# Soft mixture of experts: transposes of x issued from ScalarE's queue, kept operands stored when made

## The chip, the cores and the metric

The kernel runs on one core of a Trainium2 chip. The metric is device time in microseconds (us), from the start of the program to its end. A core has five engines that run side by side, each with its own queue in order: TensorE (PE) multiplies into PSUM, VectorE (DVE) and ScalarE (ACT) compute and empty PSUM, GpSimd (POOL) here does little but issue transfers, and SyncE (SP) only issues transfers. A transfer issued from any queue is carried out by the core's 16 DMA engines.

## The reference

```python
probs = softmax(router_logits)                 # batch 16, seq 512, 8 experts
for e in range(8):
    output += probs[:, :, e:e+1] * (x @ expert_weights[e])   # 512 x 2048 each
```

x has 8192 rows of 512 numbers, the output 8192 rows of 2048 in f32. Each row is weighted by its own probability for each expert, so the sum is one product: the row of x repeated eight times and scaled by the eight probabilities, times the eight experts' weights one above the other.

## The kernel before

That product is computed in f16 by a Strassen-like scheme of seven block products P1 to P7 at the outer level and seven steps (1, 5, 6, 2, 7, 3, 4) inside each. The rows are 32 blocks of 256 (`HQ`), 16 pairs q. The left operand of an outer product (class `Left`, L426) is made by VectorE: `times` (L422) multiplies the transposed block of x (tile xT) with the probabilities broadcast to all partitions (tile pT) into a tile z, and for some products a second such tile is subtracted. TensorE does a step as 8 matmuls of 128 x 128 against 128 x 512 (`mm`, L131). ScalarE copies step results out of PSUM (L541, L545, L548 without a base, L559 with one), VectorE adds the others (L112). In some stages ("Thirds", `run_third`, L820) two steps are split once more, with quarter-size blocks; their copies are L638 and L640.

The work is a list `stages` (L672 on) of one or two outer products each. `run(k)` (L839) goes through the slots of a stage: 7 steps by 1 or 2 products, so 14 slots in a duo stage, and 7 in the one stage that holds P6 of pair 0 alone. VectorE's work stands in a queue of tasks with costs; `slack` (L367) takes tasks off it after each step as long as its modelled clock is behind TensorE's. `need` (L357) pulls a task and all ahead of it when a step asks for its result. The order on each engine is that of the program text, held by `note` and `dve` (L100 to L108).

What concerns the change:

- **x and its transposes** (`XBlock`, L379). `begin` loads 256 rows of x from the input, cast to f16, by GpSimd's queue (tile xs, two chunks of 128 rows), for the stage two ahead, at the end of slot 1. `finish` issues two DMA transposes (L397), one for each chunk, from xs into xT; before the change it is called at the end of slot 7 for the stage two ahead (`after`, L810), from SyncE's queue. `store` writes xT to DRAM for the later passes, at the end of slot 5 of the next stage. Sixty transposes in all, in 30 blocks. Later passes load the stored xT by SyncE.
- **Kept P6 operands** (`Left.store`, L455). For the pairs q = 1 to 13 the two halves of P6's left operand, 512 KB each, are written to DRAM by SyncE and read again for P3 by ScalarE's queue. Before the change a store is issued at slots 1 and 5 of the stage in which P6 runs, which is after the operand was made.
- **SyncE's queue** also has the loads of pT and of stored xT, and the base tiles h (earlier partial sums from the DRAM tiles kept, or from the output). **GpSimd's queue** has the casts of x and of the weights, the parts of weight sums that VectorE builds (wd), and the output stores. **ScalarE's queue** has whole weight tiles (L166) and the kept operands (L492), besides its copies.
- **Pools.** xs, xT and pT share one ring of 9 tiles, the h tiles one of 13; PSUM has 8 banks. A new tile waits until the last use of the buffer that it takes.
- **Semaphores.** Transfers from the hardware queues (SyncE's and ScalarE's together) take eight semaphores in turn in the program's order; a transfer waits until the one before it on its semaphore has landed.

Of the kernel before, what the change touches and what calls it, by code (L numbers as in the profile page):

```python
# [31 lines left out]
def kernel(  # L32
# [7 lines left out]
    nc = tc.nc  # L40
    P = 128
# [337 lines left out]
    class XBlock:  # L379
# [12 lines left out]

        def finish(self):
            if self.xs is not None:
                self.t = xpool.tile([P, C, HQ], f16, name="xT", tag="x")
                for j in range(HQ // P):
                    note(nc.sync.dma_start_transpose(out=self.t[:, :, ds(j * P, P)], in_=self.xs[:, j, :]))  # L397
                self.xs, self.new = None, True

# [6 lines left out]
    class PBlock:  # L406
# [9 lines left out]

        def finish(self):
            pass

        store = finish  # L420

# [4 lines left out]
    class Left:  # L426


        def __init__(self, xb, pb, less=None, of=None, part=None):
            self.xb, self.pb, self.less, self.of, self.part = xb, pb, less, of, part  # L430
            self.t, self.task, self.s2, self.i = [None, None], {}, None, None

# [25 lines left out]
        def queue_make(self, k):  # L458
            for make in self.makes(k):
                self.task[k] = later(1.14, make)  # L460

        def queue_s2(self):
# [303 lines left out]

    def finish_loads(stage):
        if stage < len(stages):
            for p in stages[stage]:
                for load in p.loads:  # L770
                    load.finish()

# [37 lines left out]
    def after(stage, n):  # L810
        if n == 1:
            queue_lefts(stage + 1)
        if n == late.get(stage, 1):
            start_loads(stage + 2)
        if n == 5:
            store_loads(stage + 1)
        if n == 7:
            finish_loads(stage + 2)

# [345 lines left out]
    for q in KEEP:  # L1165
        for k, slot in enumerate((1, 5)):
            at(k5 + 1 + q, slot, lambda q=q, k=k: lefts[6, q].store(k))
        at(k3 + (q - 1) // 2, 8 + 3 * ((q - 1) % 2), lambda q=q: lefts[3, q].part.fetch())
# [14 lines left out]
    store_loads(0)  # L1183
    finish_loads(1)
    for k in range(len(stages)):
# [29 lines left out]
```

## Time and profile before

| | |
|---|---|
| median of 3 runs | 1379.85 us (1375.95 to 1384.18) |
| the profiled execution's own time | 1372.54 us |
| its span in the profile | 1370.8 us |
| granted TensorE clock | 1.0 |
| transfers | 358.50 MB |
| GpSimd's queue (q0), share of the 16 DMA engines | 56.1% |
| SyncE's queue (q1) | 31.3% |
| ScalarE's queue (q10) | 8.3% |

The profile is of one execution. "Busy" is the time in which an engine carried out instructions; those that only issue transfers are listed under the engine's name with a q (SPq, ACTq), and are not busy time. A row of a timeline has start, duration, engine, source line, operation, tiles (out<-in) and a count, and in brackets the idle time before it with what ended it. A row of the waits has total, number and the longest. Line numbers are those of the kernel before.

### The profile page before, as it was taken

The numbers are of one execution on the slowest core, as the hardware profiler recorded it, in microseconds if no ns is written. First come the engines' busy times: TensorE is split into PE (matmuls) and PEld (weight loads), VectorE is DVE, ScalarE is ACT, GpSimd is POOL, SyncE is SP. The second block draws the span as 40 slices with busy tenths as digits, with TensorE's granted clock in tenths as the row PEclk, the third lists the DMA queues.
The fourth block names the chain that finished last, engine by engine and source line by source line (L and its number), as shares of the span: only waits on it lengthen the run. The fifth ranks groups of instructions, "written<-read, shape, count | busy, mean of one in ns | idle before, by whom it ended". The sixth has DMA issues, their size and how long they took to land.

```text
span 1370.8 us, 18076 instructions
## 1 busy us (share of the span) xinstructions
PE 1362.6 (99%) x6610; PEld 644.1 (47%) x6610; DVE 1121.1 (82%) x1359; ACT 193.7 (14%) x354; POOL 411.4 (30%) x652
## 2 busy tenths in 40 slices
PE   8999999999999999999999999999999999999999
PEld 4455444444444444444444444444444444456554
DVE  5868757689889888798887978888889798997873
ACT  3232111100011111111111100000000000123321
POOL 3222333331223343343332112242332422233232
PEclk9999999999999999999999999999999999999999
DMA  9898999999897999999998999889797979999896
GB/s 182 217 223 245 208 237 283 233 323 358 235 340 245 323 295 332 286 318 315 306 296 289 364 371 258 200 236 209 227 264 216 242 212 282 309 209 241 203 207 121
DMA packets 193161, 358.50 MB, mean 262 GB/s; under 512 B 53168, under 2 KB 87216, under 8 KB 187696
## 3 DMA queue, kind: packets, MB, share of 16 engines
q0 software_dynamic: 88688, 185.12, 56.1%
q1 hardware_dynamic: 98336, 130.15, 31.3%
q10 hardware_dynamic: 6048, 42.08, 8.3%
q8 instruction: 51, 0.84, 0.2%
q14 instruction: 38, 0.31, 0.1%
HBM read 214.47 MB, written 170.07 MB: 281 GB/s over the span
## 4 chain that ended last, share of the span: by engine, by line
PE 74%; issue 11%; DMA 9%; POOL 4%; DVE 1%; ACT 0%; SPq 0%; POOLq 0%; DVEq 0%
PE ps L132 74%; DMA out_dram<-h 4%; POOL out_dram L126 2%; DMA wd<-w 2%; DMA xs<-in_x_dram 2%; DMA xT<-xs 1%; POOL wd L126 1%; POOL w L126 1%; DMA w<-in_expert_weights_dram 0%; DVE h L112 0%; DVE z L112 0%; POOL xs L126 0%; SPq L397 0%; POOLq L126 0%; DVE z L234 0%
## 5 line engine op out<-in xcount | busy, mean ns | idle before, releaser
L132 PE MATMUL ps<-w,z 128*128 128x512 f16 (+1 forms) x5272 | 1136.1, 376 | 1.7 <-DMA w<-in_expert_weights_dram 1.2
L132 PEld LDWEIGHTS <-z 128*128 128x128 f16 x5344 | 522.7, 98 | 607.2 <-DVE h L112 1.5
L126 POOL DMA_DIRECT2D out_dram<-h x380 | 249.1, 661 | 722.6 <-ACT h L559 365.4
L112 DVE TENSOR_TENSOR h<-ps,h 128x512 f32<-128x512 f32 x415 | 283.1, 686 | 177.1 <-PE ps L132 159.2
L112 DVE TENSOR_TENSOR z<-xT,pT 128x2048 f16<-128x2048 f16 x220 | 266.8, 1216 | 13.8 <-DMA xT<-xs 11.4
L132 PE MATMUL ps<-w,d 128*128 128x512 f16 x880 | 199.1, 379 | 0.4 <-DVE ps L112 0.4
L132 PEld LDWEIGHTS <-d 128*128 128x128 f16 x880 | 86.1, 98 | 102.5 <-issue 0.7
L112 DVE TENSOR_TENSOR z<-z,d 128x2048 f16<-128x2048 f16 x110 | 131.5, 1215 | 0.0
L112 DVE TENSOR_TENSOR w<-w 128x1024 f16<-128x1024 f16 (+2 forms) x92 | 100.7, 1102 | 9.2 <-DMA wd<-w 5.0
L559 ACT COPY h<-ps 128x512 f32<-128x512 f32 x64 | 37.5, 586 | 480.6 <-PE ps L132 458.8
L548 ACT COPY h<-ps 128x512 f32<-128x512 f32 x90 | 52.8, 586 | 326.5 <-PE ps L132 292.4
L112 DVE TENSOR_TENSOR d<-z 128x1024 f16<-128x1024 f16 x110 | 74.7, 686 | 7.6 <-PE ps L132 6.0
L112 DVE TENSOR_TENSOR ps<-ps,h 128x512 f32<-128x512 f32 (+1 forms) x102 | 60.3, 595 | 19.5 <-PE ps L132 19.3
L545 ACT COPY h<-ps 128x512 f32<-128x512 f32 x90 | 52.0, 589 | 151.7 <-PE ps L132 148.8
L126 POOL DMA_DIRECT2D wd<-w x86 | 48.6, 587 | 45.5 <-DVE w L112 34.7
L126 POOL DMA_DIRECT2D w<-in_expert_weights_dram x65 | 48.4, 761 | 28.0 <-DMA wd<-w 17.9
L126 POOL DMA_DIRECT2D kept<-h x56 | 30.8, 549 | 70.3 <-ACT h L548 40.0
L112 DVE TENSOR_TENSOR z<-z,u 128x2048 f16<-128x2048 f16 x38 | 46.1, 1214 | 0.1
L112 DVE TENSOR_TENSOR u<-xT,pT 128x2048 f16<-128x2048 f16 x38 | 46.2, 1215 | 0.0
L112 DVE TENSOR_TENSOR h<-h 128x512 f32<-128x512 f32 (+2 forms) x69 | 45.0, 674 | 0.1
L541 ACT COPY ps<-ps 128x512 f32<-128x512 f32 x45 | 25.6, 570 | 104.0 <-PE ps L132 98.2
L112 DVE TENSOR_TENSOR z<-z 128x2048 f16<-128x2048 f16 x32 | 39.0, 1220 | 0.6
(60 smaller groups left out, 262.8 us busy)
## 6 DMA issues: line engine op xcount, KB each, us to landing
out_dram<-h POOLq DMA_DIRECT2D x380, 256.0 KB, 6.7
pT<-p_dram SPq DMA_DIRECT2D x127, 256.0 KB, 6.5
w<-wd ACTq DMA_DIRECT2D x27, 1024.0 KB, 9.2
h<-kept SPq DMA_DIRECT2D x100, 256.0 KB, 7.9
xT<-x SPq DMA_DIRECT2D x74, 256.0 KB, 6.6
wd<-w POOLq DMA_DIRECT2D x72, 256.0 KB, 6.2
w<-in_expert_weights_dram POOLq DMA_DIRECT2D x35, 512.0 KB, 9.5
h<-out_dram SPq DMA_DIRECT2D x68, 256.0 KB, 5.5
```

The source lines that it names most:

```text
L112: dve(nc.vector.tensor_tensor(out=o, in0=a, in1=b, op=op))
L126: note(nc.gpsimd.dma_start(out=o, in_=i, **how))
L132: note(nc.tensor.matmul(ps, z, w, start=start, stop=stop, skip_group_check=True))
L541: act(nc.scalar.copy(self.banks["b"], x))
L545: act(nc.scalar.copy(o[tn], q if p == 5 else x))
L548: act(nc.scalar.copy(o[TN[p]], b if p == 2 else x))
L559: act(nc.scalar.copy(o[tn], b))
```

## The change

`finish` issues the transposes one chunk at a time and takes the queue that issues them, ScalarE's unless told otherwise; only the opening's four stay on SyncE's. The first chunk goes out at the end of slot 9 and the second at the end of slot 11 in a duo stage, at 5 and 7 in a stage of one product; before, both went out at the end of slot 7. The store of a kept P6 half becomes a task of cost 0 in VectorE's task queue right behind the one that makes it, so that it is issued where the operand is made.

```diff
-        def finish(self):
+        def finish(self, j, begin=nc.scalar):
             if self.xs is not None:
-                self.t = xpool.tile([P, C, HQ], f16, name="xT", tag="x")
-                for j in range(HQ // P):
-                    note(nc.sync.dma_start_transpose(out=self.t[:, :, ds(j * P, P)], in_=self.xs[:, j, :]))
-                self.xs, self.new = None, True
+                if j == 0:
+                    self.t = xpool.tile([P, C, HQ], f16, name="xT", tag="x")
+                note(begin.dma_start_transpose(out=self.t[:, :, ds(j * P, P)], in_=self.xs[:, j, :]))
+                if j == HQ // P - 1:
+                    self.xs, self.new = None, True
...
         def queue_make(self, k):
             for make in self.makes(k):
                 self.task[k] = later(1.14, make)
+            if self.kept is not None:
+                self.task[k] = later(0.0, lambda: self.store(k))
...
-        if n == 7:
-            finish_loads(stage + 2)
+        first = 9 if len(stages[stage]) == 2 else 5
+        if n in (first, first + 2):
+            finish_loads(stage + 2, (n - first) // 2)
...
-        for k, slot in enumerate((1, 5)):
-            at(k5 + 1 + q, slot, lambda q=q, k=k: lefts[6, q].store(k))
...
-    finish_loads(1)
+    for j in range(HQ // P):
+        finish_loads(1, j, nc.sync)
```

In the order of instructions of the two programs, TensorE, VectorE and GpSimd have the same instructions in the same order. ScalarE gains 56 transposes, SyncE loses them, and SyncE's kept stores stand earlier among its loads.

More of the change, by code (lines that the diff above doesn't have):

```diff
@@ L415, in begin, with finish, store @@
                 sp(self.t, p_dram[self.h, ds(self.first, HE), :].partition_broadcast(P))
-        def finish(self):
+        def finish(self, *how):
             pass
-        store = finish
+        def store(self):
+            pass
     def times(z, k, xb, pb):
@@ L430, in __init__ @@
             self.xb, self.pb, self.less, self.of, self.part = xb, pb, less, of, part
-            self.t, self.task, self.s2, self.i = [None, None], {}, None, None
+            self.t, self.task, self.s2, self.i, self.kept = [None, None], {}, None, None, None
         def makes(self, k):
@@ L765, in start_loads, with finish_loads @@
                     load.begin()
-    def finish_loads(stage):
+    def finish_loads(stage, *how):
         if stage < len(stages):
@@ L770, in finish_loads @@
                 for load in p.loads:
-                    load.finish()
+                    load.finish(*how)
     def store_loads(stage):
```

## Prediction

> **What bounds the kernel now.** I read the page's first part, then TensorE's timeline and its own waits, and only then the queue that the change empties.
>
> ```profile
> span 1370.8 us, 18076 instructions
> PE 1362.6 (99%) x6610; PEld 644.1 (47%) x6610; DVE 1121.1 (82%) x1359; ACT 193.7 (14%) x354; POOL 411.4 (30%) x652
> ```
>
> TensorE is busy for 1362.6 of 1370.8 us. A busy TensorE may still run below its rate, so the next view is its timeline, in one steady stage (14 steps of 8 matmuls) and in the one place where gaps stand.
>
> ```profile
> 640.37 3.62 PE L132 MATMUL ps<-w,d 128*128 128x512 f16 x16
> ...
> 664.54 3.62 PE L132 MATMUL ps<-w,d 128*128 128x512 f16 x16
> ...
> 810.15 3.62 PE L132 MATMUL ps<-w,d 128*128 128x512 f16 x16 [0.41 <-DVE ps L112]
> ```
>
> A stage of 112 matmuls takes 664.54 - 640.37 = 24.17 us, 216 ns a matmul; the row of 16 keeps that rate (16 x 216 ns = 3.46 us, and the tail of the last makes 3.62). A bracket is idle time: none stands in the steady stage, and 0.41 us at 810. The whole list of TensorE's waits:
>
> ```profile
> PE ps L132 <- ACT h L331: 1.4, 1, 1.4
> PE every L94 <- DVE zero L91: 1.3, 1, 1.3
> PE ps L132 <- DMA w<-in_expert_weights_dram: 1.2, 1, 1.2
> PE ps L132 <- DVE h L112: 0.5, 1, 0.5
> PE ps L132 <- DVE ps L112: 0.4, 1, 0.4
> ```
>
> Columns: us in total, times, longest. The first three lie in the opening, before any step that the diff touches. The last two, 0.5 + 0.4 = 0.9 us, come at 810 to 818 us. This is the first bound of the forecast: the change moves no matmul and no VectorE instruction (in the order of instructions, TensorE's, VectorE's and GpSimd's lists are the same before and after), so **in this execution it can give back at most 0.9 us**, 0.07%.
>
> Now SyncE's queue, which the change empties: its wait at the transposes, and the view of line 397 (durations in ns, and how long the transposes took to land).
>
> ```profile
> SPq L397 <- DMA xs<-in_x_dram: 242.5, 23, 17.4
> ```
> ```profile
> L397 SPq DMA_TRANSPOSE xT<-xs x60: 1191/1266/2277, 47.5 to 722.5; - x60
> ...
> DMA to landing us min/median/max: 2.4/6.4/11.3
> ```
>
> SyncE stood 242.5 us at its transposes until the x rows had come, with all its later loads behind it. Yet TensorE waited for none of those loads: the 242.5 us lie beside matmuls.
>
> **The change part by part.**
>
> *Transposes leave SyncE (56 of 60; the first four stay).* Removed there: 56 x 1.266 = 71 us of issuing and the 242.5 us of waiting. On the path: nothing, by the list of TensorE's waits. Cover: the matmuls of the stage. If that cover were thin, the loads queued behind would be late and TensorE's list would show it; after the opening it shows the 0.9 us at 810 alone, past the last transpose (722.5). So 0.
>
> *They go to ScalarE, 2 or 4 at a time.* Added there: 56 x 1.266 = 71 us of issuing on an engine that is busy for 193.7, plus a wait at the head of an in-order queue. What stands behind it: the copies that empty PSUM. I take the worst steady stage that I found, the one in which the rows of x come latest against ScalarE (ScalarE, then SyncE):
>
> ```profile
> 647.47 0.59 ACT L548 COPY h<-ps 128x512 f32<-128x512 f32 x1 [1.14 <-PE ps L132]
> 657.83 0.59 ACT L548 COPY h<-ps 128x512 f32<-128x512 f32 x1 [9.77 <-PE ps L132]
> 661.34 0.57 ACT L541 COPY ps<-ps 128x512 f32<-128x512 f32 x1 [2.92 <-PE ps L132]
> ```
> ```profile
> 651.97 3.17 SPq L397 DMA_TRANSPOSE xT<-xs  x2
> ```
>
> The new transposes stand between the copies of 647.47 and 657.83, in a hole of 9.77 us. ScalarE reaches them at 648.06, waits until 651.97 (3.9 us; SyncE starts there as soon as the rows land), issues two in 2 x 1.266 = 2.5 (3.17 at SyncE) and is free at 654.5 to 655.2, before its next copy at 657.83. Even past that there is room: the first result that TensorE needs is the copy of 661.34, for the second half of the 664.54 row (8 matmuls later, 664.54 + 1.73 = 666.27). Taking off two copies and the issue, 666.27 - 0.57 - 0.59 - 2.5 = 662.6: the rows may land 14.5 us after ScalarE gets there, and land 3.9 after. Price 0.
>
> The tight case is the Third stages near the start, with four transposes and a shorter tail:
>
> ```profile
> 81.36 0.59 ACT L548 COPY h<-ps 128x512 f32<-128x512 f32 x1 [1.14 <-PE ps L132]
> 89.20 0.36 ACT L638 COPY ps<-ps 128x256 f32<-128x256 f32 x1 [7.25 <-PE ps L132]
> ```
> ```profile
> 79.78 14.11 SPq L397 DMA_TRANSPOSE xT<-xs  x4
> ```
> ```profile
> 75.23 1.23 DVE L112 TENSOR_TENSOR z<-xT,pT 128x2048 f16<-128x2048 f16 x1 [6.35 <-DMA xT<-xs]
> ```
>
> 4 x 1.266 = 5.1 us in a hole of 7.25: from 81.95 to 87.0, 2.2 us to spare. Price 0. VectorE gains: SyncE's four took 14.11 us here, with waits between them, where ScalarE takes 5.1; the last row shows VectorE idle for 6.35 us for such a result one stage earlier, which should shrink. It is idle time of VectorE that TensorE did not see, so 0 too.
>
> *Moved later.* In the earlier duo stages SyncE issued its pair ahead of ScalarE's hole; the farthest that I found:
>
> ```profile
> 118.65 3.02 SPq L397 DMA_TRANSPOSE xT<-xs  x2
> ```
> ```profile
> 128.12 0.59 ACT L548 COPY h<-ps 128x512 f32<-128x512 f32 x1 [1.14 <-PE ps L132]
> ```
> ```profile
> 144.48 1.21 DVE L112 TENSOR_TENSOR z<-xT,pT 128x2048 f16<-128x2048 f16 x1
> ```
>
> The pair goes out 10 us later, from 128.71, is issued by 131.2 and lands 6.4 us (median) to 11.3 us (longest) after: 137.6 to 142.5. The first VectorE product that reads it starts at 144.48. Price 0, with 2 us left in the worst case; the store of x and the loads behind it on SyncE are off the path as above.
>
> *Kept P6 operands.* 26 stores of 512 KB, as many as before, now sent when VectorE has made them and not at slots 1 and 5 of the next stage. They get a lane partner: transfers from SyncE's and ScalarE's queues take eight semaphores in turn, and each waits until the last one on its semaphore has landed. The order of instructions with its waits shows that in five stages the second transpose of a pair follows a kept store in this way.
>
> ```profile
> DMA to landing us min/median/max: 4.5/10.3/15.4
> ```
> ```profile
> 592.69 1.23 DVE L112 TENSOR_TENSOR z<-z 128x2048 f16<-128x2048 f16 x1
> ```
> ```profile
> 609.49 0.59 ACT L548 COPY h<-ps 128x512 f32<-128x512 f32 x1 [9.77 <-PE ps L132]
> ```
>
> (The first row is the kept stores', from the view of that tile; then VectorE and ScalarE.) In the latest of the five the operand is ready at 593.9; with the median the store lands at 604.2, with the longest at 609.3, while ScalarE's next copy is at 609.49 and may be some 7 us late unpunished (above: 666.27 - 0.57 - 0.59 - 657.83 = 7.3). Bounds: 0, and 1.3 us of late issue that the same 7 us hide. I take 0. On SyncE the store now waits for VectorE ahead of the base loads; those are added to a product some slots later, and the matmuls cover them again.
>
> *Sum:* -0.9 to 0 against the execution's own 1372.54 us (span 1370.8 and 1.7 around it). I take 0. The runs shown are slower, 1375.95 to 1384.18 with a median of 1379.85, 7.3 above it. No trace shows what those 7.3 us are. With nothing of the sum pointing elsewhere I carry them over: 1379.85 less some of the 0.9, **1379 us**, "no change" within the 0.5% (6.9 us) that a measurement of this kernel can tell.
>
> **The rivals.**
>
> *Slower: the third queue slows GpSimd's transfers.* GpSimd's queue shares the DMA engines with SyncE's; transposes on ScalarE's queue make a third claimant while a pair lands. The place is the stages from 575 to 660 us, where the parts of weights come through GpSimd and VectorE is the one just in time:
>
> ```profile
> 581.32 1.42 DVE L112 TENSOR_TENSOR w<-w 128x1024 f16<-128x1024 f16 x2 [3.97 <-DMA wd<-w]
> ...
> 590.84 0.69 DVE L112 TENSOR_TENSOR ps<-ps,h 128x512 f32<-128x512 f32 x1
> ```
> ```profile
> 592.02 3.62 PE L132 MATMUL ps<-w,d 128*128 128x512 f16 x16
> ```
> ```profile
> DVE w L112 <- DMA wd<-w: 5.0, 3, 4.0
> DVE w L112 <- DMA w<-in_expert_weights_dram: 2.5, 2, 1.8
> ```
> ```profile
> w<-wd POOLq DMA_DIRECT2D x12, 256.0 KB, 5.5
> w<-in_expert_weights_dram POOLq DMA_DIRECT2D x12, 256.0 KB, 9.6
> ```
>
> After a wait of 3.97 us VectorE ends at 591.53 what TensorE uses at 592.02: 0.49 us of margin. If the claimants share evenly and a half becomes a third, a landing of 5.5 or 9.6 us (these two rows are of 480 to 730 us) grows by half, 2.75 to 4.8. VectorE waited for such transfers 3 and 2 times; 3 x 2.75 + 2 x 4.8 = 17.9 us if TensorE feels all, nothing if the pairs miss them. It decides as soon as a part lands over 0.5 us later. Estimate 9, so **1388**. Against it: the transposes' bytes are the same, and in the stage quoted above the pair goes out at its old time, since it waits for the x rows in both kernels; only its company changes.
>
> The Trainium skill, "DMA: Bandwidth & Descriptors", Queues, rings and completion order, has each DMA engine take turns between the queue rows that have work, a packet at a time; by that rule three claimants get a third each, and this rival's time would hold. The same page, under Issuing engines are not separate DMA queues, says that issuing from several engines saves the sequencer's time alone; by it the gain would be SyncE's 71 us of issuing, none of it on the path, and the forecast's time would stand.
>
> *Faster: the runs' 7.3 us are SyncE's late loads.* If the loads behind 242.5 us of waiting are what comes late in executions without a profile, they go, and the kernel falls to its floor: 1372.54 - 0.9 = 1371.6 at best, **1372.5** here. For it: something does vary between executions, and this is the second longest wait in SyncE's list. Against it: TensorE's list has none of it.
>
> *The fixed places are not what holds them.* Where x rows land after ScalarE arrives (651.97 against 648.06), arrival times the transposes in both kernels, and nothing moves: the time of before, **1379.85**.
>
> ScalarE held at the head of its queue also happens in before, where the price can be read:
>
> ```profile
> 795.68 0.59 ACT L559 COPY h<-ps 128x512 f32<-128x512 f32 x1 [14.88 <-DMA w<-wd]
> ```
>
> 14.88 us behind a weight load that it had to issue, and TensorE lost 0.9 us after it at most. A blocked ScalarE is cheap here.
>
> **How the numbers follow.** Forecast 0.57, fixed places that hold nothing 0.11, third queue 0.20, floor 0.10, ScalarE blocked by rows over 14.5 us late 0.02. Within 0.5%: 0.57 + 0.11 = 0.68. Faster by over 0.5% (below 1372.95): 0.10. Slower by over 0.5%: 0.20 + 0.02 = 0.22. The likeliest one's own range is that of the runs, 1376 to 1384. The range that should hold 8 in 10 takes in the floor, 1371.5, and the lower half of the slower rival up to its estimate, 1388.
>
> **What would show it.** Right: TensorE's waits still below 5 us and 24.2 us a steady stage; transposes on ScalarE's queue starting 0 to 10 us later than on SyncE's; no wait of SyncE for xs after the first four; ScalarE's copies after them waiting for TensorE still; VectorE's waits for xT below 11.4 us. Wrong: idle brackets on TensorE between 575 and 660 us with a VectorE releaser that waited for GpSimd's transfers (third queue), brackets released by ScalarE (blocked queue), or timed runs near 1372 (floor).

## The result, and the profile after

The changed kernel takes 1395.94 us in the median of 4 runs (1390.73 to 1400.11), the kernel before on the same chip 1377.9 (4 runs, 1374.63 to 1384.18): ratio 1.0137, 95% interval 1.0111 to 1.0163. That is 18 us slower, outside the predicted range of 1371.5 to 1388. The profiled execution of the changed kernel took 1393.44 us with a span of 1391.7; before it was 1372.54 and 1370.8, so the two profiles differ by 20.9 us. Lines after the change are a few higher: L552 is the copy that was L548, L642 and L644 those that were L638 and L640.

The page's first part, and TensorE's waits (total, times, longest):

```profile
PE 1366.1 (98%) x6610; PEld 644.2 (46%) x6610; DVE 1120.5 (81%) x1359; ACT 193.6 (14%) x354; POOL 412.3 (30%) x652
```
```profile
PE ps L132 <- DVE h L112: 13.4, 5, 8.7
PE ps L132 <- ACT h L644: 3.0, 1, 3.0
PE ps L132 <- DVE ps L112: 2.7, 2, 1.9
```

VectorE and ScalarE do the same work in the same time; TensorE is busy 3.5 us longer with the same matmuls and waits 19.1 us outside the opening where it waited 0.9 (17.6 of them as idle time in brackets). Its timeline says where (start, duration, idle before in the bracket):

```profile
91.89 2.76 PE L132 MATMUL ps<-w,z 128*128 128x512 f16 x16 [1.71 <-DVE h L112]
...
590.85 8.79 PE L132 MATMUL ps<-w,z 128*128 128x512 f16 x40 [1.34 <-DVE h L112]
...
625.92 3.61 PE L132 MATMUL ps<-w,d 128*128 128x512 f16 x16 [1.95 <-DVE ps L112]
...
653.54 10.52 PE L132 MATMUL ps<-w,z 128*128 128x512 f16 x48
672.72 13.29 PE L132 MATMUL ps<-w,z 128*128 128x512 f16 x48 [8.66 <-DVE h L112]
```

Two places: the stages before 320 us (1.71 and 0.77 us around 92, 3.00 at 315), and 590 to 672 us. The largest stop costs more than its 8.66 us: the 48 matmuls behind it take 13.29 us where those ahead of it take 10.52. The view by stretches shows the clock (the column of its own after POOL; then the share of the DMA engines and GB/s):

```profile
672.00:690.00 18.00, 17.28 (x68) 7.26 (x68) 15.91 (x21) 2.24 (x4) 4.51 (x8) 0.82 0.93 245
690.00:702.00 12.00, 12.00 (x57) 5.40 (x56) 8.53 (x13) 1.26 (x3) 4.32 (x8) 1.00 1.01 293
```

The 0.82 is a mean of two: in shorter stretches of the same view the granted clock is 1.00 from 664 to 668 us, 0.51 from 668 to 678 and 1.00 from 680 to 690. So it was halved 4 us into the stop, for 10 us. The Trainium skill, "TensorE: Matmul & The Clock Gate", Part 1: The HAM clock gate, says that an idle window of some 3.4 us drops the clock; the 8.66 us stop agrees with it, and the stops of under 2 us above, and the one of 3.00 us, brought no longer matmuls. In e8, below, a stop of 2.35 us was once enough.

What VectorE waited for, and what GpSimd's queue did ahead of it:

```profile
664.66 0.69 DVE L112 TENSOR_TENSOR w<-w 128x1024 f16<-128x1024 f16 x1 [6.97 <-issue]
668.70 0.69 DVE L112 TENSOR_TENSOR w<-w 128x1024 f16<-128x1024 f16 x1 [3.35 <-DMA w<-in_expert_weights_dram]
671.38 0.69 DVE L112 TENSOR_TENSOR w<-w 128x1024 f16<-128x1024 f16 x1 [1.98 <-DMA w<-in_expert_weights_dram]
```
```profile
649.84 0.54 POOL L126 DMA_DIRECT2D out_dram<-h  x1 [6.77 <-DMA wd<-w]
653.52 0.54 POOL L126 DMA_DIRECT2D out_dram<-h  x1 [3.14 <-DMA wd<-w]
656.90 0.72 POOL L126 DMA_DIRECT2D w<-in_expert_weights_dram  x1 [2.83 <-DMA wd<-w]
657.61 0.56 POOL L126 DMA_DIRECT2D w<-wd  x1
```

The sums of weights at 664 to 672 us need parts that GpSimd loads. It issued them from 656.90 on, because its queue had stood 6.77 + 3.14 + 2.83 us until earlier stores of parts had landed. In the kernel before the same loads go out without such waits:

```profile
634.54 0.54 POOL L126 DMA_DIRECT2D out_dram<-h  x1 [1.08 <-ACT h L548]
635.10 0.72 POOL L126 DMA_DIRECT2D w<-in_expert_weights_dram  x1
```

So the chain is: GpSimd's transfers land late, its queue stands, the parts come late, VectorE is late, TensorE stops. The landing times of the issues between 480 and 730 us, before and then after (KB each, median us from issue to landing):

```profile
out_dram<-h POOLq DMA_DIRECT2D x85, 256.0 KB, 7.3
wd<-w POOLq DMA_DIRECT2D x40, 256.0 KB, 6.6
xT<-xs SPq DMA_TRANSPOSE x20, 6.5
```
```profile
out_dram<-h POOLq DMA_DIRECT2D x78, 256.0 KB, 10.1
wd<-w POOLq DMA_DIRECT2D x38, 256.0 KB, 9.1
xT<-xs ACTq DMA_TRANSPOSE x20, 13.9
```

The stop of 1.71 us at 92 us has another chain: VectorE waits for xT. ScalarE took 10.42 us to issue the four transposes of the stage before, and VectorE's products of them stood 9.43 us, where the longest such wait before the change was 6.35:

```profile
57.60 10.42 ACTq L397 DMA_TRANSPOSE xT<-xs  x4
```
```profile
77.37 2.54 DVE L112 TENSOR_TENSOR z<-xT,pT 128x2048 f16<-128x2048 f16 x2 [9.43 <-DMA xT<-xs]
...
91.15 2.48 DVE L112 TENSOR_TENSOR h<-ps,h 128x512 f32<-128x512 f32 x4
```

VectorE's tasks behind it come late, down to the four sums at 91.15, which stood at 87.68 before; the first of them ends the stop. ScalarE stood too, for the next four:

```profile
81.70 10.83 ACTq L397 DMA_TRANSPOSE xT<-xs  x4
92.63 0.36 ACT L642 COPY ps<-ps 128x256 f32<-128x256 f32 x1 [10.48 <-DMA pT<-p_dram]
```

The view of line 397 from 80 to 95 us gives the four issues 1250, 1844 and 3582 ns (shortest, median, longest) and one wait at a semaphore 2074 ns: 8.5 us of the 10.83 are the issues themselves. TensorE ran on from 91.89, ahead of the copy at 92.63, so this stand didn't hold it. Nor do transposes stand in the stop at 315 us: ScalarE issues none between 285 and 320 us, and its copy there waits 5.17 us (2.16 before) for an output store of GpSimd's.

```profile
314.57 0.37 ACT L644 COPY h<-ps 128x256 f32<-128x256 f32 x1 [5.17 <-DMA out_dram<-h]
```

### The profile page after: what moved, and what is told of

The parts are those of the page before. It is cut to its first block, busy times and chain, and to the rows that moved or that the text cites. A ratio compares the mean times of both kernels' runs of the same rounds, so it can differ in the third digit from the quotient of the medians.

```text
span 1391.7 us, 18104 instructions
## 1 busy us (share of the span) xinstructions
PE 1366.1 (98%) x6610; PEld 644.2 (46%) x6610; DVE 1120.5 (81%) x1359; ACT 193.6 (14%) x354; POOL 412.3 (30%) x652
## 4 chain that ended last, share of the span: by engine, by line
PE 61%; DMA 18%; issue 14%; POOL 5%; DVE 2%; ACT 0%; ACTq 0%; POOLq 0%; SPq 0%; DVEq 0%
PE ps L132 61%; DMA out_dram<-h 5%; DMA wd<-w 5%; POOL out_dram L126 2%; DMA w<-in_expert_weights_dram 2%; DMA pT<-p_dram 1%; DMA w<-wd 1%; POOL w L126 1%; DMA wd<-u 1%; DMA xT<-xs 1%; DVE h L112 1%; POOL wd L126 1%; DMA kept<-h 1%; DMA w<-in_x_dram 0%; POOL xs L126 0%
## 5 line engine op out<-in xcount | busy, mean ns | idle before, releaser
L112 DVE TENSOR_TENSOR z<-xT,pT 128x2048 f16<-128x2048 f16 x220 | 267.2, 1218 | 15.0 <-DMA xT<-xs 13.3
L552 ACT COPY h<-ps 128x512 f32<-128x512 f32 x90 | 52.7, 587 | 343.3 <-PE ps L132 239.5
L112 DVE TENSOR_TENSOR ps<-ps,h 128x512 f32<-128x512 f32 (+1 forms) x102 | 60.4, 597 | 21.1 <-PE ps L132 20.8
```

The source lines that it names most:

```text
L112: dve(nc.vector.tensor_tensor(out=o, in0=a, in1=b, op=op))
L552: act(nc.scalar.copy(o[TN[p]], b if p == 2 else x))
```

## The experiments

The theories. **1**: the transposes, as a third stream of their own, delay GpSimd's transfers. **2**: SyncE, no longer standing for xs, sends its loads earlier, and these delay GpSimd's. **3**: the earlier kept stores do it. **4**: ScalarE, standing at its transposes for rows or semaphores, delays its copies and the rest. Theory 5 came at the end: it is the transposition itself.

Besides the times, one row per profile tells where each lost its time: the 335 copies of ScalarE come in the same order in all kernels, so the start of a copy against its start in the kernel before (profile against profile) is how late the kernel is by then. Each row is one execution: the profiled one of the kernel before took 1372.54 us, under its median of 1377.9, and those of e3 and e7 took 7 us more than the medians of e3 and e7.

| lateness in us at (time of before) | 110 | 340 | 580 | 610 | 660 | 740 | 1355 |
|---|---|---|---|---|---|---|---|
| after | 2.9 | 5.9 | 6.1 | 7.5 | 21.2 | 21.6 | 20.8 |
| e3, new places, SyncE | 2.6 | 2.5 | 4.3 | 15.7 | 15.7 | 15.7 | 15.3 |
| e7, kept stores on ScalarE | 0.5 | 3.1 | 6.6 | 7.5 | 11.9 | 12.6 | 13.3 |
| e9, even blocks on ScalarE | 4.8 | 5.4 | 5.4 | 15.0 | 15.0 | 15.0 | 13.9 |
| e10, odd blocks on ScalarE | 4.1 | 3.9 | 4.5 | 5.9 | 19.4 | 19.4 | 19.5 |
| e11, SyncE held | 4.9 | 10.6 | 11.7 | 18.5 | 20.8 | 26.1 | 25.7 |
| e12, an eighth kept | 4.2 | 7.1 | 7.1 | 8.9 | 8.9 | 8.9 | 32.1 |
| e13, all on SyncE, new | 2.0 | 1.9 | 2.2 | 1.9 | 7.7 | 7.7 | 7.5 |
| e14, plain copies, ScalarE | 0.7 | 0.5 | 0.5 | 0.3 | 0.3 | 0.3 | 1.2 |
| e16, an eighth kept, same reads | 3.8 | 4.7 | 6.5 | 6.7 | 6.7 | 6.7 | 8.0 |
| e17, plain copies, SyncE | 2.7 | 2.6 | 3.2 | 2.9 | 2.9 | 2.9 | 3.4 |
| e18, half plain | 1.4 | 1.3 | 1.3 | 4.2 | 4.2 | 5.8 | 5.9 |

### The change taken apart: e1 to e4

**e1**: the changed kernel with the kept stores at their old slots. **e2**: the kernel before with the kept stores behind the task that makes them, and nothing else. **e3**: transposes at the new places, but from SyncE's queue, kept stores old. **e4**: transposes from ScalarE's queue, both at the old slot 7, kept stores old.

```diff
@@ e3, against e1 @@
-        def finish(self, j, begin=nc.scalar):
+        def finish(self, j, begin=nc.sync):
@@ e4, against the kernel before @@
-        def finish(self):
+        def finish(self, begin=nc.scalar):
...
-                    note(nc.sync.dma_start_transpose(out=self.t[:, :, ds(j * P, P)], in_=self.xs[:, j, :]))
+                    note(begin.dma_start_transpose(out=self.t[:, :, ds(j * P, P)], in_=self.xs[:, j, :]))
...
-    finish_loads(1)
+    finish_loads(1, nc.sync)
```

> The transposes go out from ScalarE's queue at the new slots; the kept stores stay at slots 1 and 5 as before. Theory 1 (third queue: with transposes in ScalarE's queue GpSimd's transfers land later, 7.3 to 10.1 us for output stores between 480 and 730 us, and VectorE gets its weight parts late): slower, 1388 to 1396 us, output stores at 9 us or more in that stretch. Theory 2 (SyncE freed of its 242.5 us of waiting sends its loads into the time of GpSimd's): slower too, by as much. Theory 3 (the kept stores, sent early, are what collides): same as before, 1372 to 1384.

Measured 1392.5 us (10 runs), ratio 1.0092 (1.0058 to 1.0125). Two thirds of the loss are there without the earlier stores.

> Only the kept stores are sent when made; all transposes stay on SyncE at slot 7. Theories 1 and 2: same as before, 1372 to 1384 us, output stores at about 7.3 us between 480 and 730 us. Theory 3: slower, 1388 to 1396.

Measured 1376.08 us, ratio 0.9978 (0.9953 to 1.0002). Theory 3 falls: alone, the stores cost nothing.

> The transposes go out at the new slots, one chunk each, but from SyncE's queue; kept stores as before. Theory 1 (it is the queue): same as before, within 0.5%. Theory 2 (it is SyncE's wait that is lost): part of the loss, since SyncE reaches the transposes later and waits for x less, 240 us down to under 100; 1382 to 1390 us.

Measured 1381.2 us, ratio 1.0017 (0.9988 to 1.0045). On SyncE's queue the new places cost nothing that can be told, though the profiled execution (1387.88 us) had 8.7 us of stops around 595 us. It also has the stop at 92 us (1.45 us), and so have e6 and e13 (1.45 each), with every transpose on SyncE's queue; e2, e4 and e7, at the old places, have none there. That stop goes with the new places (e9 alone has them without it), not with ScalarE's queue.

> The transposes go out from ScalarE's queue at the old slot 7, both chunks together; kept stores as before. Theory 1: slower like the changed kernel, 1388 to 1396 us. Theory 2: the same. If ScalarE standing at the head of its queue were the cause (theory 4), slower than with the new slots, over 1400, with TensorE's idle time released by ScalarE.

Measured 1407.36 us (4 runs), ratio 1.019 (1.0129 to 1.0252). The old place does not help; so it is the queue. It is more than theory 1 had (1388 to 1396), and what e4 loses above e1 isn't explained. TensorE's waits in e4:

```profile
PE ps L132 <- DVE ps L112: 11.2, 3, 9.6
PE ps L132 <- DVE h L112: 10.3, 5, 4.8
PE ps L132 <- ACT h L641: 3.0, 1, 3.0
```

Most of it is VectorE again, and ScalarE, the engine that the transposes were put on, has 3.0 us. Theory 4 had the time (over 1400) but not the engine.

### SyncE set free? e5 and e6

**e5** is e1 with SyncE sending 16 bytes of xs to a scratch tensor at slot 7, so that it stands for xs as before. **e6** has the transposes on SyncE's queue, both at the end of slot 11.

```diff
@@ e5, against e1 @@
+        def touch(self):
+            if self.xs is not None:
+                sp(dram.tile([1, 8], f16, name=f"scr_{self.h}"), self.xs[0:1, 0, 0:8])
...
+        if n == 7 and stage + 2 < len(stages):
+            for p in stages[stage + 2]:
+                for load in p.loads:
+                    load.touch()
@@ e6, against e3 @@
-        first = 9 if len(stages[stage]) == 2 else 5
-        if n in (first, first + 2):
-            finish_loads(stage + 2, (n - first) // 2)
+        if n == (11 if len(stages[stage]) == 2 else 7):
+            for j in range(HQ // P):
+                finish_loads(stage + 2, j)
```

> As e1 (transposes from ScalarE's queue, kept stores as before), and SyncE again waits for the x rows at slot 7: it sends 16 bytes of them to DRAM, for each block. That gives back the hold on SyncE's later loads that the change took away. Theory 1 (third queue): still slow, 1385 to 1396 us, TensorE's idle time over 10 us. Theory 2 (SyncE's loads set free): back to before, 1373 to 1384, with SyncE's wait for xs over 200 us again.

Measured 1411.94 us (4 runs), ratio 1.0252 (1.0209 to 1.0295). SyncE's wait is back:

```profile
SPq L123 <- DMA xs<-in_x_dram: 201.6, 25, 14.1
```

and the time is not: theory 2 falls. Its premise was thin as well, since SyncE stands after the change as it did before, at other places: 628.8 us for VectorE's z (424.3 before) and 149.6 for xT (42.9), with 1.6 for xs (242.5). Why e5 is slower than e1, SyncE's standing or the turns of its extra transfers on the semaphores, isn't separated.

> The transposes stay on SyncE's queue, both at slot 11, when the x rows have mostly landed; kept stores as before. SyncE's wait for xs should fall well under the 242.5 us of before. Theory 1: no third queue, so about as before, 1373 to 1385 us (some loss where the transposes land too late is possible). Theory 2: slower by as much as e1, 1388 or more, the more the wait falls.

Measured 1381.03 us, ratio 1.0026 (1.0007 to 1.0045). The expected fall of SyncE's wait did not come (205.7 us still), so it says only that the places cost little on this queue, 0.3%.

### A third stream, and more time for the sums: e7 and e8

**e7** is the kernel before with the 26 kept stores issued from ScalarE's queue: a third stream of plain transfers in the same stretch. **e8** is the changed kernel with the sums of parts due later.

```diff
@@ e7, against the kernel before @@
-            sp(self.kept[:, k], self.t[k])
+            note(nc.scalar.dma_start(out=self.kept[:, k], in_=self.t[k]))
@@ e8, against the changed kernel @@
-    by_parts(k5 + 2, 4, 14, 7, load_part("t3"), None, (7,))
+    by_parts(k5 + 2, 4, 14, 7, load_part("t3"), None, (11,))
-    by_parts(*slots_after(k5 + 2, 4, 60), 24, 4, load_p4, less_t2, (8, 15))
+    by_parts(*slots_after(k5 + 2, 4, 60), 24, 4, load_p4, less_t2, (12, 20))
```

> The kernel before, with the 26 kept stores (512 KB each, operands long made) sent from ScalarE's queue in place of SyncE's; transposes on SyncE. A third claimant in the stretch from 480 to 730 us without a transpose in it. Theory 1 in its general form (any third queue takes its share from GpSimd's): slower, 1383 us or more, output stores of that stretch from 7.3 to 9 us or more. If only transposes in a queue of their own do it (theory 1b): as before, 1372 to 1384, output stores near 7.3.

Measured 1378.52 us, ratio 1.0006 (0.9983 to 1.0029). Its rows between 480 and 730 us:

```profile
q10 hardware_dynamic: 2760, 10.06, 11.0%
...
out_dram<-h POOLq DMA_DIRECT2D x80, 256.0 KB, 9.4
```

ScalarE's queue carries four times the bytes that the transposes have there (10.06 MB against 2.36), and the median is that of before. The profiled execution is the longest of its ten (1385.85 us): in it GpSimd's stores land almost as late as after the change and TensorE stands 3.27 us before 556.89, and four of the ten took over 1382 us, as did one of 19 of the kernel before. So a third stream of any kind is not the 18 us, and theory 1 in its general form falls as their account; that it costs something now and then isn't excluded. 1b, a third stream of transposes, is left.

> The changed kernel, with VectorE's sums of the weight parts queued 4 to 5 slots later after their loads (7 to 9 us), the loads themselves where they were. If the late parts on GpSimd's queue are what stops TensorE between 575 and 690 us: most of the idle time there goes, some 12 of 17 us, and 4 us of slow matmuls after it: 1376 to 1386 us. If TensorE's stops have other causes: still 1390 or more.

Measured 1399.95 us (4 runs), ratio 1.0172 (1.0134 to 1.0209). The stops moved (2.34 at 484.93, 2.35 at 511.61, 2.35 at 538.28, 3.39 at 657.97, 2.93 at 749.04) and the loss stayed: what is short is not the time of one sum.

### Which half, and holding SyncE: e9 to e12

The even blocks of x (P1's) are transposed up to about 430 us, the odd ones (P5's) from about 445 us on. **e9** keeps only the even ones on ScalarE's queue, **e10** only the odd ones. **e11** holds SyncE until both transposes have landed. **e12** stores an eighth of each kept half.

```diff
@@ e9, against the changed kernel @@
+                begin = nc.scalar if self.h % 2 == 0 else nc.sync
                 note(begin.dma_start_transpose(out=self.t[:, :, ds(j * P, P)], in_=self.xs[:, j, :]))
@@ e10, against the changed kernel @@
+                begin = nc.scalar if self.h % 2 else nc.sync
@@ e11, against the changed kernel @@
+                    if begin is nc.scalar:
+                        sp(dram.tile([1, 8], f16, name=f"scr_{self.h}"), self.t[0:1, 0, ds(P - 4, 8)])
@@ e12, against the changed kernel @@
-            sp(self.kept[:, k], self.t[k])
+            sp(self.kept[:, k, 0:1], self.t[k][:, 0:1])
...
-            note(nc.scalar.dma_start(out=self.t, in_=self.source))
+            note(nc.scalar.dma_start(out=self.t, in_=self.source[:, :, 0:1].to_broadcast([P, 2, K8, HQ])))
```

> The changed kernel, but only the even blocks of x (those of P1, transposed up to about 430 us) are transposed from ScalarE's queue; the odd blocks (those of P5, from about 445 us on) stay on SyncE's, at the new places. If the loss is made where the transfers of the weights' parts are late for VectorE (theory 1: the stops at 590 to 672 us), nearly all of it is gone: 1380 to 1385 us, ratio 1.001 to 1.005, with only the stops at 92 and 315 us left (2.5 and 3.0 us). If ScalarE's own standing at the semaphores of its transposes makes the loss (theory 4: lanes), half of the transposes leave about half of it: 1387 us, ratio 1.007.

Measured 1386.41 us, ratio 1.0067 (1.0046 to 1.0087). Above what theory 1 had, and near theory 4's half. The table shows why the reading "half" would be wrong too: the profile's 9.6 us at 580 to 610 us come where all transposes are on SyncE's queue, at the new places. The edit also reaches the opening's four transposes, which the changed kernel leaves on SyncE's queue, and there ScalarE does stop TensorE, so e9 overstates the early half by up to that:

```profile
53.25 5.30 PE L132 MATMUL ps<-w,d 128*128 128x512 f16 x16 [2.80 <-ACT ps L546]
```

> The other half: only the odd blocks (P5's, from about 445 us on) are transposed from ScalarE's queue, the even ones from SyncE's. Theory 1: nearly the whole loss stays, 1390 to 1395 us, ratio 1.009 to 1.013, with VectorE's stops of TensorE between 480 and 750 us. Theory 4: about half, 1387 us.

Measured 1392.57 us (4 runs), ratio 1.0106 (1.0077 to 1.0136). As theory 1 had it, with the same stop as after the change:

```profile
671.42 12.81 PE L132 MATMUL ps<-w,z 128*128 128x512 f16 x48 [10.48 <-DVE h L112]
```

> The changed kernel, with SyncE sending 16 bytes of xT to a scratch tensor behind each pair of transposes, so that its queue stands until they have landed and starts nothing beside them; GpSimd's and ScalarE's queues are as in the changed kernel. If the transposes cost because they run beside SyncE's transfers as a third stream (theory 1b), they land in 7 to 8 us instead of 13.9 between 480 and 730 us, GpSimd's stores in 8 instead of 10.1, and the time is back at 1378 to 1385 us. If it is their place on ScalarE (lanes, its copies), it stays at 1392 to 1400. If SyncE's bursts after a wait are what hurts (the reading of the 1411.94 us of the kernel in which SyncE still waited for xs), it is 1400 to 1415.

Measured 1395.64 us (4 runs), ratio 1.0128 (1.0095 to 1.0161). Making SyncE stand until the transposes have landed does not bring the time back, and GpSimd's stores take 9.4 us between 480 and 730 us, not 8. SyncE now stood 434.4 us for xT, which may cost something of its own, so this run alone doesn't clear SyncE's transfers.

> The changed kernel, with an eighth of each kept P6 half stored (it leaves the rest out, and P3 reads the eighth eight times over, so its operand isn't the reference's): some 12 MB less through SyncE's queue between 450 and 790 us, where the 16 DMA engines are full (share 1.02 to 1.10 in each window). Transposes from ScalarE's queue stay as they are. If the loss comes from a DMA system that is full in this stretch (theory 1), the landing times fall (transposes under 10 us, GpSimd's stores under 8.5) and the stops between 480 and 750 us go: 1374 to 1382 us. If it comes from ScalarE's waits or the semaphores in turn, which don't hang on the bytes, it stays at 1390 to 1396.

Measured 1407.95 us, ratio 1.0212 (1.0184 to 1.0239), outside both. The table has the reason: from 340 to 740 us this kernel lost only 1.8 us (the stop at 660 is gone), and from 1150 us on it lost 24 in its own P3 reads in short pieces. e16 does it without those. The landing times between 480 and 730 us did not fall as expected: 13.1 us for the transposes and 8.9 for GpSimd's stores.

### The transposition itself: e13 to e18

**e13**: the changed kernel with every transpose on SyncE's queue (default `begin=nc.sync`). **e14**: a plain copy of the same 128 KB for each of the 56 transposes, from ScalarE's queue. **e17**: the same copies from SyncE's queue. **e18**: only the second of each pair plain, ScalarE's queue. **e16**: an eighth of the kept halves of pairs 2 to 13, P3 reading pair 1's whole operand. **e15**: e2 again, five rounds.

```diff
@@ e14, against the changed kernel @@
-                note(begin.dma_start_transpose(out=self.t[:, :, ds(j * P, P)], in_=self.xs[:, j, :]))
+                if begin is nc.scalar:
+                    note(begin.dma_start(out=self.t[:, :, ds(j * P, P)],
+                                         in_=self.xs[:, j, :].rearrange("p (c t) -> p c t", c=C)))
+                else:
+                    note(begin.dma_start_transpose(out=self.t[:, :, ds(j * P, P)], in_=self.xs[:, j, :]))
@@ e16, against the changed kernel @@
+            n = slice(0, 1 if self.light else K8)
+            sp(self.kept[:, k, n], self.t[k][:, n])
...
-            return Left(xblock(a), pt, part=Operand(lefts[6, q].kept)), [xblock(a), pt]
+            return Left(xblock(a), pt, part=Operand(lefts[6, 1].kept)), [xblock(a), pt]
...
+                left.light = q > 1
```

> The changed kernel with every transpose left on SyncE's queue: new places and earlier kept stores together. If the loss is all in ScalarE's queue, this is the sum of the two parts run alone (1.0017 and 0.9978): 1374 to 1382 us, ratio 0.998 to 1.003. If the places and the stores hurt together (the stop at 597 us in the kernel with the early blocks on ScalarE), it is 1384 to 1388, ratio 1.005 to 1.008, and ScalarE's queue is left with the rest.

Measured 1383.32 us, ratio 1.0036 (1.0018 to 1.0054), between the two expectations: places and stores together do cost about 5 us on SyncE's queue, in a stop of 3.90 us at 660 in the profile. The rest, 1.0137 against 1.0036, is ScalarE's queue, and the halves add up within their intervals: e9 0.0031 (with the opening's stop in it) and e10 0.0070 above e13, together 0.0101.

> The changed kernel with each of the 56 transposes on ScalarE's queue replaced by a plain copy of the same 128 KB from xs to xT in pieces of 256 bytes (it leaves the transposition out). If any small transfer in a queue of its own, beside two full ones, slows the others, or if ScalarE's standing at the semaphores does it, the loss stays: 1390 to 1398 us. If it is what a transpose asks of the DMA engines, the loss goes: 1376 to 1384 us, GpSimd's stores land in under 8.5 us and the copies in under 8 between 480 and 730 us.

Measured 1373.97 us, ratio 0.9965 (0.9951 to 0.998). **The whole loss goes**, and a little more. The copies land sooner than the transposes did, but not by much: in 7.6 us against 10.3 (median over the run), in 11.2 against 13.9 between 480 and 730 us. More changed for the others, here between 480 and 730 us:

```profile
out_dram<-h POOLq DMA_DIRECT2D x85, 256.0 KB, 6.9
wd<-w POOLq DMA_DIRECT2D x40, 256.0 KB, 6.7
```

The stop at 315 us is gone as well, and that at 92 us is down to 0.65. ScalarE issues four in 4.63 us and then waits for TensorE, as before the change.

```profile
81.64 4.63 ACTq L398 DMA_DIRECT2D xT<-xs  x4
89.34 0.36 ACT L646 COPY ps<-ps 128x256 f32<-128x256 f32 x1 [7.25 <-PE ps L132]
```

A copy also takes less issuing than a transpose (median 644 ns against 1324 on ScalarE's queue), so e14 changes ScalarE's time too. Between 480 and 730 us that is not the cause: after eight of the changed kernel's ten pairs there, ScalarE's next copy waits for TensorE, and the stops come through VectorE.

> The kept stores alone, the transposes as before, in more rounds (0.9978 the first time, 0.9953 to 1.0002). As forecast, nothing: 0.997 to 1.002. If stores issued earlier and landing in 6.8 us instead of 11.6 give SyncE's later loads room, 0.995 to 0.998: then it is the version that beats both.

Measured 1376.87 us (12 runs), ratio 0.9992 (0.9974 to 1.001). No difference; with 0.9978 the first time, a gain isn't shown.

> The changed kernel with an eighth of each kept P6 half stored for the pairs 2 to 13, and P3 reading pair 1's whole operand for all (it leaves the rest out; the reads of the last third stay as they are). 11 MB less for the DMA engines between 460 and 790 us. If the loss there comes from engines that are full, only the early stops stay: 1377 to 1385 us, ratio 1.000 to 1.006. If it comes from the semaphores in turn or from ScalarE standing, 1390 to 1397 us.

Measured 1381.13 us, ratio 1.0029 (1.0006 to 1.0051). With 11 MB less to carry, the transposes on ScalarE's queue cost little after the early stages (4.7 us by 340 in the profile, 2.0 from there to 740). So the loss after 480 us hangs on the bytes that stand beside the transposes. The share of the DMA engines doesn't tell it: it is 1.00 from 480 to 730 us in e16, 1.03 after the change. GpSimd's stores still land in 9.5 us, so late stores alone aren't the loss either.

> The kernel with all transposes on SyncE's queue at the new places and the earlier kept stores (1.0036), with the 56 replaced by plain copies of the same bytes in pieces of 256 bytes (it leaves the transposition out). Theory 5: as fast as the plain copies from ScalarE's queue or a little slower, since SyncE still waits for xs: 1372 to 1377 us, ratio 0.995 to 0.999, and the rate while they are under way at 300 GB/s or more. If the copies on SyncE's queue stop its loads as the transposes do, the 1383 us stay: the gain of the plain copies then came from ScalarE's queue.

Measured 1373.97 us, ratio 0.9991 (0.9979 to 1.0003). Against e14's 0.9965 (the chips differ, so the ratios are what can be compared) SyncE's queue is 0.0026 worse, not better: for plain copies the queue makes no difference of the size in question, 0.0101 the other way.

> The changed kernel with the second transpose of each block replaced by the plain copy, both on ScalarE's queue (it leaves half of the transposition out). Theory 5: the time with transposes under way halves, to some 60 us of the 250, and with it the loss between 0.9965 and 1.0137: 1382 to 1387 us, ratio 1.003 to 1.007. If the stops come as soon as any transpose stands beside two busy queues, it stays above 1390; if only pairs back to back are dear, it is under 1379.

Measured 1378.33 us, ratio 1.0028 (1.0007 to 1.0048), under the expected 1382 to 1387: half the transposes make (1.0028 - 0.9965) / (1.0137 - 0.9965) = 37% of the loss. That is less than half, but with the three intervals a half isn't excluded; what is shown is that the loss doesn't come all at once.

What a transposition does to the others can be read from how many bytes all queues together moved while the 256-byte pieces of the pairs were under way (from the first piece to the last; pieces less than 1.5 us apart are one stretch), between 480 and 730 us. First the kernel before, ten stretches (and one between two of them), then after, nine, then e14, ten; two or one of each are shown, and the sum of their lengths; the last column is GB/s:

```profile
554.50:563.40 8.90, 8.90 (x43) 4.04 (x42) 6.45 (x10) 0.59 (x1) 3.48 (x7) 1.00 1.23 191
575.00:579.50 4.50, 4.50 (x23) 2.03 (x22) 2.35 (x4) 0.28 (x1) 2.67 (x5) 1.00 1.11 185
...
sum 48.60, PE 48.60 PEld 22.02 DVE 35.06 ACT 2.48 POOL 23.22; mean PE 4.86 PEld 2.20 DVE 3.51 ACT 0.25 POOL 2.32
```
```profile
563.40:575.00 11.60, 11.60 (x56) 5.27 (x54) 10.73 (x13) 2.64 (x5) 1.27 (x2) 1.00 1.06 372
```
```profile
513.50:528.00 14.50, 14.50 (x69) 6.55 (x67) 11.49 (x17) 1.75 (x3) 5.05 (x9) 1.00 1.04 336
...
558.90:574.10 15.20, 15.20 (x72) 6.89 (x71) 13.59 (x18) 1.25 (x3) 5.89 (x10) 1.00 1.16 229
590.10:600.40 10.30, 9.55 (x45) 4.36 (x45) 9.64 (x14) 1.74 (x3) 3.99 (x8) 1.00 1.11 176
...
sum 108.20, PE 105.51 PEld 47.31 DVE 87.78 ACT 12.68 POOL 36.72; mean PE 11.72 PEld 5.26 DVE 9.75 ACT 1.41 POOL 4.08
```
```profile
603.90:616.40 12.50, 12.50 (x60) 5.65 (x58) 10.46 (x15) 1.16 (x2) 5.04 (x9) 1.00 1.07 364
...
sum 102.90, PE 102.90 PEld 46.65 DVE 86.44 ACT 9.80 POOL 38.63; mean PE 10.29 PEld 4.66 DVE 8.64 ACT 0.98 POOL 3.86
```

The DMA share stands above 1.0 in every stretch shown. The stretches differ much: 185 to 294 GB/s before, 176 to 336 after, 274 to 391 in e14. Their rates, weighted with their lengths, and the rest of the 250 us from the mean of the whole:

| | under way, us of 250 | GB/s meanwhile | GB/s in the rest | all of the 250 us |
|---|---|---|---|---|
| transposes, SyncE's queue (before) | 48.6 | 232 | 325 | 307 |
| the same, earlier kept stores (e15) | 66.2 | 231 | 332 | 305 |
| the same, new places too (e13) | 76.6 | 229 | 339 | 305 |
| transposes, ScalarE's queue (after) | 108.2 | 274 | 302 | 290 |
| plain copies, SyncE's queue (e17) | 43.0 | 346 | 304 | 311 |
| plain copies, ScalarE's queue (e14) | 102.9 | 350 | 287 | 313 |

The same bytes in the same pieces run at 346 to 350 GB/s without a transposition and at 229 to 274 with one, whichever queue issues them. With places and stores alike, a queue of its own makes the pairs of transposes take 1.4 times as long (76.6 to 108.2) and the plain copies 2.4 times (43.0 to 102.9). For the plain copies that is harmless.

For the transposes it would be a simple account that everything runs slower for longer, but the figures don't bear it out. Against the plain rate, before leaves 48.6 x (346 - 232) = 5.5 MB undone, e15 66.2 x (346 - 231) = 7.6, e13 76.6 x (346 - 229) = 9.0 and after 108.2 x (350 - 274) = 8.2. Yet e15 loses nothing and e13 5 us, where the change loses 18. The bytes left undone are an estimate of what a transposition takes from the others, not of what the kernel loses by it; that hangs on which transfers are late, and GpSimd's stores, 7.3 us before and 8.3 in e15, 8.7 in e13, 10.1 after, are only a sign of it.

The Trainium skill, "Advanced Engine Details and Errata", X-Bar Transpose (TRN2), has transposing transfers on this chip "as fast as regular DMAs". For their own landing on SyncE's queue that is nearly so here (median 7.5 us in e13, 7.3 for the copies of e17), but not on ScalarE's (10.3 against 7.6), and not for the kernel: with the 56 transposes made plain, the ratio falls from 1.0036 to 0.9991 on SyncE's queue and from 1.0137 to 0.9965 on ScalarE's. The measurement decides.

What stays open: what a transposition does inside the DMA engines (no view of the profile shows it), why a queue of its own makes it cost 18 us rather than 5, why new places and earlier stores cost 1.0036 together and 1.0017 and 0.9978 alone, how much of e5 and e11 is SyncE's standing, and why e4 is slower than e1. Of the kernels that leave nothing out none is shown to beat the kernel before; e2 is the part of the change that can be kept (0.9978 and 0.9992), at no gain that can be told.

## Why the prediction was wrong, point by point

- **TensorE bounds, at most 0.9 us to win**: right. So was *transposes leave SyncE: 0*, though its wait mostly moved: 242.5 us for xs became 1.6, and its waits for VectorE's z and for xT grew by 204.5 and 106.7. TensorE got nothing for it.
- **"They go to ScalarE ... Price 0": the step that failed**, in what it counted. It priced ScalarE's time: the issue, the hole between copies, the room of 14.5 us. In the steady stages that holds (2.6 to 4.7 us a pair, most of them in holes of 9.8). It put at nothing what the transposes do to other transfers once they stand in a queue of their own, since the number of bytes is the same. The runs put 0.0101, about 14 us, on just that: 1.0137 against 1.0036 for the same transposes, places and stores on SyncE's queue (e13), and nothing of it is left with plain copies on ScalarE's (e14, 0.9965). A pair is under way for 12.0 us there, for 7.7 in e13 and for 4.9 before, GpSimd's stores land in 10.1 us, and the chain through its late parts stops TensorE. How the queue does it stays open. The DMA engines had little to spare there, as the view by stretches of the kernel before tells in its last but one column, and the prediction didn't read it:

```profile
480.00:560.00 80.00, 80.00 (x372) 36.24 (x371) 65.49 (x85) 10.51 (x18) 30.84 (x55) 1.00 1.02 300
560.00:640.00 80.00, 79.90 (x371) 36.18 (x370) 70.02 (x89) 11.66 (x20) 29.99 (x52) 1.00 1.07 321
640.00:730.00 90.00, 90.00 (x419) 40.78 (x418) 74.76 (x96) 12.85 (x22) 29.13 (x52) 1.00 1.04 302
```

  That share alone doesn't mark the place: it is 1.06 from 200 to 300 us too, where the change lost nothing. It takes a consumer that is just in time as well, which the prediction had found, VectorE's sums from 575 us on.
- **The Third stages, "4 x 1.266 = 5.1 us in a hole of 7.25"**: wrong in size. It took 10.83 us, because the four issues took 8.5 on ScalarE and waited 2.07 besides; SyncE's own 14.11 us "with waits between them" in the quoted row was a warning. But TensorE didn't wait for it.
- **"VectorE gains", "should shrink", 0**: wrong the other way. The wait of 6.35 us became 9.43, and TensorE did see it, 1.71 us at 92. The 3.00 us at 315 are an output store's, and why it landed late isn't shown.
- **"Moved later ... 2 us left in the worst case"**: the landing of 6.4 us (11.3 at most) was that of SyncE's queue at the old places. It became 10.3 (19.9), and VectorE's waits for xT, forecast to fall below 11.4, are 13.3. The stop at 92 us is this step's, since e3, e6 and e13 have it on SyncE's queue.
- **Kept P6 operands: 0**: right (0.9978 and 0.9992); they land in 6.7 us where they took 11.6 between 480 and 730 us.
- **The slower rival** had the place (575 to 660 us; the stop ends at 672), the engine just in time, and the chain through GpSimd's transfers. Its size was half: 9 us by its estimate, 18 measured. That its bound was 17.9 is luck: the 18 have stops from before 480 us and the lowered clock in them, which it didn't count. Its reason was wrong, even shares among three claimants: e7 and e14 have three and lose nothing in the median. "Only its company changes" was given against it, and that was what cost.
- **The two rules on queues**. The Trainium skill, "DMA: Bandwidth & Descriptors", Issuing engines are not separate DMA queues, has it that issuing from another engine saves the sequencer's time alone. That holds here for the plain copies (0.9965 and 0.9991 from the two queues) and not for the transposes (1.0137 and 1.0036). The Trainium skill, "DMA: Bandwidth & Descriptors", Queues, rings and completion order, has the engines take turns between queue rows; pairs that take 1.4 and 2.4 times as long in a row of their own agree with that, but turns alone made no loss.
- **"A blocked ScalarE is cheap here"**: in the stage at 82 us it was, after a stand of 10.83 us; in the opening it wasn't (2.80 us in e9).

## What to carry to other kernels

Moving a transfer to an idle queue moves no bytes, but it changes how long the transfer is under way and what runs beside it. So look for the stretches where the DMA engines are busy throughout and a consumer is just in time, and don't price the move there by the queue that issues it alone. A transposing DMA is dearer than its bytes for everything beside it, and here it was cheaper behind its neighbours in one queue than as a stream of its own. And test a suspected transfer by putting a plain one of the same size in its place, in both queues. Last, check an account by figures on a kernel that loses nothing: bytes left undone fitted the change and failed on e15.

## What the runs showed of the hardware that was not expected

- While transposing DMAs are under way, all queues together move 229 to 274 GB/s in the mean between 480 and 730 us; beside plain copies of the same 256-byte pieces it is 346 to 350.
- Issuing a transpose took ScalarE 1324 ns in the median and up to 3582, a plain copy of the same pieces 644.
- A stop of 8.66 us costs 11.4: the clock was half for 10 us from 4 us into the stop, and 48 matmuls took 13.29 us, not 10.52. In e8 one stop of 2.35 us halved it too (80 matmuls at 538.28 took 19.05 us), while two as long, at 484.93 and 511.61, did not (17.43).
- Sending 16 bytes a block, to make a queue stand where it stood before, cost 1.0252 against 1.0092; whether by the standing or by the turns of these transfers on the semaphores isn't shown.
